# mLSTM state update, token scores and memory attention of a hybrid decoder step: ScalarE decay, grouped column-tiled products, zero-padded 64-row operands

## The chip, the cores and the metric

The kernel runs on one core of one Trainium2 chip. The metric is the time of one execution on the device, in microseconds (us); the median of three runs stands for a kernel. One profiled execution, with a record of every instruction, gives the views that are quoted below.

## The reference

One layer of a decoder serves 512 prompt rows and 8 decoding sequences of 4 new tokens each (32 sample rows) with the same weights; d_model is 1024 and everything is fp32. Cut to what matters here:

```python
# 1. hybrid mixer: mLSTM heads (4 x 128) beside differential attention (4 heads; q, k = 2 x 64, v = 128)
z = rms_norm(x) @ w_in
C_new = decay * C + (w * k)^T v          # mLSTM state, per sequence and head, 128 x 128
num   = w_inter * (q @ C) + s @ v        # the cached state is read before it is replaced
s     = einsum('bqhcd,bkhcd->bhcqk', q, k) * 64 ** -0.5      # c = 0, 1: two components of 64
p     = softmax(where(causal, s, -inf)); a = p[c=0] - lam * p[c=1]; o = a @ v
#    prompt: 512 keys; each sequence: 256 paged keys (2 pages) + its 4 new ones
x = x + rms_norm(concat(h_ml, h_da) @ w_out)
# 2. cross-attention, 4 heads x 256, into 256 memory tokens
#    prompt: k, v = mem_prompt @ w_mk, w_mv; each sequence: its own cached k, v (1 MB each)
x = x + rms_norm(softmax(q @ k^T / 16) @ v @ w_mo)
# 3. ConvFFN, d_ff = 2752 = 21.5 x 128
x = x + rms_norm((silu(g) * a) @ w_down)     # a, g: causal width-3 convolutions of x @ w_up
```

It returns the layer's output and the new caches and states.

## The kernel before, in words

**Units and queues.** TensorE (PE) does products and transposes, VectorE (DVE), ScalarE (ACT) and GpSimd (POOL) the rest; nearly all loads and stores are issued on one queue, SP's. The program is written in a tile framework: tiles come from pools with a fixed number of buffers, a new tile waits until its buffer's last user is done, and a planner orders each engine's instructions ahead of time from the program's order and its own estimate of when each becomes ready. `tc.issue_after(x)` holds the instructions in its block behind instruction x.

**Pools that the change touches.** S has 11 large tiles (transposed queries and keys, probabilities, padded operands). W has 4 slots of 128x2x1024; a slot holds one split weight tile, or one sequence's transposed keys (kT), or its values (vt). Stage (wst) has 6 buffers of 128x1024 for what is loaded. PSUM is shared by a pool of five banks (names mm, sda, ssc, tpa, oda, sca) and one of three (tpk, mlus, mlsi, cpt, spa and other short-lived results). T2, Z and N hold temporaries.

**Weights.** Each product with weights is done as three passes with operands split into a high and a low part: ACT casts the staged tile to the high part, DVE subtracts it for the low one (`split`, lines 142 and 143). `W.add` notes weight tiles in program order, `W.pump` loads and splits as many as there are slots (`W.nslots`), `W.get` and `W.free` pass them on. `slotA` makes a tile of 256 rows x 512 columns; the last 192 rows of w_down come as 128 and 64 rows, each split by itself.

**mLSTM states of the sequences (L948 to L964).** Step i of 8 is group g = i // 4 of four sequences and head i % 4. At the first step of a group, 16 products (32 query columns each, in one of four column tiles of PE) read that group's states into `pi` (mlsi). Then one matmul gives the four sequences' updates (mlus, 128x512), four DVE instructions do state = state * decay + update, and the state tile is stored. The state tiles sit in buffers that later stages load into.

**Token attention (L1139 to L1189 and the loop behind it).** For each sequence b, `dk_load` gathers two pages of keys, `dk_turn` transposes them (two tpk banks, one copied by ACT and one by DVE), `dk_scores` does four passes, one for each head, in column tiles of 32, and then the row maximum (DVE) and exp (ACT). Queries of both components lie side by side, zero-padded, in `qz`. A pipeline runs the three with one step of prompt attention between each two.

**Prompt attention.** `da_soft(i)` is block b = i // 4 of 128 queries and head i % 4. Component c lies in partitions 64c to 64c + 63 of `dqT` and `dkT`; its scores are one fp32 product over these 64 rows (two passes) and a bf16 matmul that adds the causal mask:

```python
rr = slice(64 * c, 64 * c + 64)
mm(sv[c], lhsT=dqT[rr, h, c0:c0 + P], rhs=dkT[rr, h, 0:nk], start=True, stop=False)
mm(sv[c][:, c0:nk], lhsT=identb, rhs=cmaskb, start=False, stop=True)
```

Maximum (DVE), exp (ACT) and the combination of both components (DVE) follow; `da_turn` transposes, `da_av` multiplies with the values. Fillers (`F`) with other work run between the steps.

**Memory attention (L1373 to L1450).** A half load i is 128 of a sequence's 256 keys, all heads. `mk_load` stages it, `mk_turn` transposes eight 128x128 blocks, `mk_scores` does a sequence's eight passes in column tiles of 32; `mv_load` loads a sequence's values into a slot of W, `mv_out` adds eight passes to `pso`. Generator `prompt` yields the prompt's own memory attention step by step: cpt and sca scores, and cpo outputs at line 1366. The order around it is written out:

```python
for b in range(NB):                  # NB = 8
    mk_scores(2 * b + 1)
    if b < 4:
        for j in (2 * b + 8, 2 * b + 9):
            mk_turn(j)
            if j + 6 < 2 * NB: mk_load(j + 6)
    else:
        mv_load(b - 4)
    if b % 2 == 1: next(prompt, None)
```

After the softmax the weight tiles of w_mo (`slotsA`, staged by line 227) are noted, sequences 4 to 7 get their `mv_load`, and `mv_out` runs from 0 to 7 with prompt steps between.

**ConvFFN.** Tiles of 128 of the 2752 features go through up projection, convolution and `gate`, then through w_down in groups; feature tile j = 21 has only 64 rows, so its products use 64 rows (`one`, L1645 to L1647, for prompt blocks; `sample_mm`, line 366, in column tiles of 32, for the sample rows).

## Time and profile before

| | |
|---|---|
| median of three runs (lowest, highest) | 990.26 us (988.76, 992.15) |
| the profiled execution, and its span | 989.55 us, 987.8 us |
| busy share of the span: PE, DVE, ACT, POOL | 97%, 61%, 39%, 20% |
| mean granted clock of TensorE | 0.993 of full speed |
| moved by DMA | 130.26 MB, 132 GB/s in the mean |

A profile line of the timeline has start and duration in us, engine, program line, operation, tile written <- tiles read, rows*columns of PE in use, shape, type, and xN where N like instructions in a row are put together; square brackets give the idle time before it and what ended that. A line of groups has busy time and mean ns of one behind the first bar, idle time before the group and its main releaser behind the second. A line by stretch has the stretch's length, then each engine's busy time and number of instructions, TensorE's granted clock, the busy share of the DMA engines and GB/s. PEld is TensorE's loading of the stationary operand, which can run beside products.

### The profile page before, as it was taken

To read this page: it belongs to the slowest core of one execution; us is meant where nothing else is said; L and a number is where in the kernel's file an instruction comes from. 1 tells how busy PE (TensorE), PEld (TensorE's weight loads), DVE (VectorE), ACT (ScalarE), POOL (GpSimd) and SP (SyncE) were. 2 spreads that over 40 slices of the span, in tenths; PEclk is the share of its full clock that TensorE was granted. 3 is DMA by queue.
4 is the path that set the end of the run, shared out by engine and by line. 5 is a ranking of instruction groups with operands and counts; after the bars stand their busy time and mean duration, and the time that the engine had idled before them with its cause. 6 is when DMAs were issued, how large, how long until landed. Compare 5 with 4: busy or idle time off the path is not lost.

```text
span 987.8 us, 17060 instructions
## 1 busy us (share of the span) xinstructions
PE 962.1 (97%) x6615; PEld 811.1 (82%) x6615; DVE 603.4 (61%) x1129; ACT 389.1 (39%) x746; POOL 195.5 (20%) x389
## 2 busy tenths in 40 slices
PE   8999999999999999999999999999999999999994
PEld 5899777789655878898767889989987997997983
DVE  6835325645786257633653569827757675685677
ACT  5754313334576357633543433342312222222232
POOL 6610000115231214400000354201100010110114
PEclk9999999999899999999999999999999999999998
DMA  8950222260835068765841764063053214304113
GB/s 283 301 161 1 86 75 91 63 206 12 255 109 177 21 219 266 261 219 168 304 171 49 233 197 127 6 171 86 4 139 103 74 42 117 118 26 141 31 47 112
DMA packets 120401, 130.26 MB, mean 132 GB/s; under 512 B 8423, under 2 KB 85832, under 8 KB 120320
## 3 DMA queue, kind: packets, MB, share of 16 engines
q1 hardware_dynamic: 114136, 125.69, 41.1%
q10 hardware_dynamic: 6184, 3.48, 1.2%
q8 instruction: 52, 0.85, 0.3%
q14 instruction: 29, 0.24, 0.1%
HBM read 112.22 MB, written 16.93 MB: 131 GB/s over the span
## 4 chain that ended last, share of the span: by engine, by line
PE 83%; DMA 6%; DVE 5%; issue 2%; ACT 2%; POOL 1%; SPq 1%; DVEq 0%; POOLq 0%; ACTq 0%
PE mm L455 30%; PE mm L386 5%; PE mm L387 5%; PE mm L388 5%; PE mm L443 5%; PE mm L1645 4%; PE mm L1647 4%; PE mm L1646 4%; PE mm L366 3%; PE sda L1180 2%; DMA xb<-x_d 2%; PE tpk L1385 2%; DMA xb<-in_x_prompt_dram 1%; DMA wst<-in_w_mk_dram 1%; PE cpo L1366 1%
## 5 line engine op out<-in xcount | busy, mean ns | idle before, releaser
L142 ACT CAST wslot<-wst 128x1024 fp32r<-128x1024 f32 (+1 forms) x127 | 131.0, 1036 | 273.3 <-issue 73.8
L455 PE MATMUL mm<-fT,wslot 128*128 128x256 f32 (+1 forms) x1872 | 235.7, 288 | 0.0
L455 PEld LDWEIGHTS mm<-fT,wslot 128*128 128x128 f32 x1872 | 234.7, 188 | 0.7 <-issue 0.4
L143 DVE TENSOR_TENSOR wslot<-wst,wslot 128x1024 fp32r<-128x1024 f32 (+1 forms) x127 | 154.9, 1222 | 91.8 <-ACT wslot L142 91.2
L1645 PE MATMUL mm<-wslot,act 128*128 128x512 f32 (+1 forms) x176 | 71.0, 405 | 0.0
L1646 PE MATMUL mm<-wslot,act 128*128 128x512 f32 (+1 forms) x176 | 69.5, 395 | 0.0
L1647 PE MATMUL mm<-wslot,act 128*128 128x512 f32 (+1 forms) x176 | 69.1, 397 | 0.0
L1546 POOL COPY cvo<-u 128x2 f32<-128x2 f32 x43 | 16.2, 377 | 221.3 <-DVE u L1544 221.3
L386 PE MATMUL mm<-wslot,hT 128*128 128x512 f32 x128 | 51.8, 407 | 0.0
L387 PE MATMUL mm<-wslot,hT 128*128 128x512 f32 x128 | 50.8, 397 | 0.0
L455 PE MATMUL mm<-hT,wslot 128*128 128x256 f32 (+1 forms) x384 | 50.7, 289 | 0.0
L388 PE MATMUL mm<-wslot,hT 128*128 128x512 f32 x128 | 50.6, 398 | 0.0
L455 PEld LDWEIGHTS mm<-hT,wslot 128*128 128x128 f32 x384 | 48.9, 188 | 0.5 <-issue 0.2
L1645 PEld LDWEIGHTS mm<-wslot,act 128*128 128x128 f32 (+1 forms) x176 | 33.4, 190 | 15.8 <-issue 7.8
L1541 DVE TENSOR_TENSOR u<-mm,rsb 128x256 f32<-128x256 f32 x43 | 18.1, 423 | 43.8 <-PE mm L455 43.8
L1647 PEld LDWEIGHTS mm<-wslot,act 128*128 128x128 f32 (+1 forms) x176 | 33.0, 188 | 7.7 <-issue 0.4
L1646 PEld LDWEIGHTS mm<-wslot,act 128*128 128x128 f32 (+1 forms) x176 | 33.1, 188 | 6.4
L1558 ACT ACTIVATE c<-c 128x560 f32<-128x560 f32 x21 | 14.1, 672 | 60.4 <-DVE c L1552 60.4
L1658 DVE TENSOR_TENSOR yp<-mm,yp 128x512 f32<-128x512 f32 x40 | 27.3, 688 | 13.7 <-PE mm L1647 13.6
L1552 DVE SCALAR_TENSOR_TENSOR c<-u,cvT,c 128x560 f32<-128x560 f32 x43 | 34.3, 797 | 0.8
L1551 DVE SCALAR_TENSOR_TENSOR c<-u,cvT,c 128x560 f32<-128x560 f32 x43 | 34.0, 792 | 0.1
L386 PEld LDWEIGHTS mm<-wslot,hT 128*128 128x128 f32 x128 | 24.1, 188 | 6.6 <-issue 2.1
(458 smaller groups left out, 1876.4 us busy)
## 6 DMA issues: line engine op xcount, KB each, us to landing
wst<-in_w_up_dram SPq DMA_DIRECT2D x42, 512.0 KB
wst<-in_w_in_dram SPq DMA_DIRECT2D x28, 512.0 KB
wst<-in_w_down_dram SPq DMA_DIRECT2D x20, 512.0 KB
wst<-in_cache_mem_k_dram SPq DMA_DIRECT2D x16, 512.0 KB
vt<-in_cache_mem_v_dram SPq DMA_DIRECT2D x8, 1024.0 KB
wst<-in_w_mk_dram SPq DMA_DIRECT2D x8, 512.0 KB
xb<-in_x_prompt_dram SPq DMA_DIRECT2D x8, 512.0 KB
wst<-in_cache_dk_dram SPq DMA_DIRECT2D x16, 256.0 KB
```

What stands on the lines that cost most here:

```text
L142: nc.scalar.copy(out=hi, in_=src)
L143: (eng or nc.vector).tensor_tensor(out=lo, in0=src, in1=f32(hi), op=SUB)
L386: mm(ps[b], lhsT=xt.hi(k, c0, c0 + n), rhs=s[:, 0, kk, :], start=(k == 0), stop=False)
L387: mm(ps[b], lhsT=xt.hi(k, c0, c0 + n), rhs=s[:, 1, kk, :], start=False, stop=False)
L388: mm(ps[b], lhsT=xt.lo(k, c0, c0 + n), rhs=s[:, 0, kk, :], start=False, stop=(k == nk - 1))
L443: mm(ps, lhsT=s[:, l, k, :], rhs=x(k, c0, c1), start=(k == 0 and j == 0), stop=(k == 7 and j == 2))
L455: mm(ps[i], lhsT=s[:, l, k, :], rhs=x(k, c0, c1), start=(k == 0 and j == 0), stop=(k == 7 and j == 2))
L1551: STT(out=c, in0=u[:, 1:EXT - 1], scalar=w[1], in1=c, op0=MUL, op1=ADD)
L1552: STT(out=c, in0=u[:, 0:EXT - 2], scalar=w[0], in1=c, op0=MUL, op1=ADD)
L1645: mm(ps, lhsT=t[:, 0, c0:c0 + P], rhs=s[:n, 0, i % 2, :], start=st, stop=False)
L1646: mm(ps, lhsT=t[:, 0, c0:c0 + P], rhs=s[:n, 1, i % 2, :], start=False, stop=False)
L1647: mm(ps, lhsT=t[:, 1, c0:c0 + P], rhs=s[:n, 0, i % 2, :], start=False, stop=en)
```

## The change

The state update reads all eight sequences' states ahead of the first update, lets ACT multiply by the decay and DVE add the whole bank. Prompt score products use all 128 rows: `dqz` is a copy of the queries with component 0's rows zero, and component 1's rows of `dqT` are cleared. Token scores are done for two sequences together, behind the second one's transposes. In the memory stage, scores of four sequences stand together twice, transposes 8 to 15 are held behind the first four, scores 4 to 7 behind the last transpose; values are loaded by halves, those of sequences 0, 1, 2 and 7 into staging buffers; outputs stand together as 0 to 3 and 4 to 7, with prompt steps between. Feature tile 21 and the last half tile of w_down are padded with zero rows to 128.

```diff
@@ -227,9 +227,10 @@
                 dma(out=st, in_=w[r0:r0 + 256, n0:n0 + 512].rearrange("(k p) n -> p k n", p=P))
                 split_w(sv, st, share)
             else:
+                nc.gpsimd.memset(st[nrow - P:, 1, :], 0.0)
                 for k, n in ((0, P), (1, nrow - P)):
                     dma(out=st[:n, k, :], in_=w[r0 + k * P:r0 + k * P + n, n0:n0 + 512])
-                    split(sv[:n, 0, k, :], sv[:n, 1, k, :], st[:n, k, :])
+                split(sv[:, 0], sv[:, 1], st)
             return sv, st
         W.add(emit)
 
@@ -948,16 +949,16 @@
     def mls_update(i):
         g, h = i // H, i % H
         cs_t = csts[g, h]
-        if h == 0:
-            for b in range(4):
+        if i == 0:
+            for b in range(NB):
                 for k in range(H):
-                    mm(pi[NS * k:NS * k + NS, 0:P], lhsT=qzm[:, 256 * k + (4 * g + b) * NS:256 * k + (4 * g + b + 1) * NS],
-                       rhs=csts[g, k][:, b, :], start=(g + b == 0), stop=(g == 1 and b == 3))
+                    mm(pi[NS * k:NS * k + NS, 0:P], lhsT=qzm[:, 256 * k + b * NS:256 * k + (b + 1) * NS],
+                       rhs=csts[b // 4, k][:, b % 4, :], start=(b == 0), stop=(b == NB - 1))
         pu = at("mlus")
         mm(pu, lhsT=kS[:, h, :], rhs=vzs[i], start=True, stop=True)
         for b in range(4):
-            STT(out=cs_t[:, b, :], in0=cs_t[:, b, :], scalar=dec[:, h, 4 + 4 * g + b:5 + 4 * g + b], in1=pu[:, b * P:(b + 1) * P],
-                op0=MUL, op1=ADD)
+            nc.scalar.mul(out=cs_t[:, b, :], in_=cs_t[:, b, :], mul=dec[:, h, 4 + 4 * g + b:5 + 4 * g + b])
+        VTT(out=cs_t, in0=cs_t, in1=v2(pu, P), op=ADD)
         dma(out=O["s_ml_C"][0, 4 * g:4 * g + 4, h].rearrange("b d e -> d b e"), in_=cs_t)
         F.run(2.5)
 
@@ -1142,6 +1143,14 @@
         rr = slice(64 * c, 64 * c + 64)
         nc.gpsimd.tensor_copy(out=qz[rr, :, :, c, :], in_=dqT[rr, :, SEQ:].rearrange("p h (g r) -> p h g r", g=2))
 
+    dqz = S([P, H, SEQ], F32, "dqz")
+    nc.gpsimd.memset(dqz[0:64], 0.0)
+    for b in range(4):
+        c = slice(b * P, b * P + P)
+        nc.scalar.copy(out=dqz[64:128, :, c], in_=dqT[64:128, :, c])
+        nc.gpsimd.memset(dqT[64:128, :, c], 0.0)
     kst, kts, pts, aTs, outs, rcs = {}, {}, {}, {}, {}, {}
 
     def dk_load(b):
@@ -1149,6 +1158,8 @@
         kst[b] = [st[:, 0:512], st[:, 512:1024]]
         for g in range(2):
             gather("cache_dk", b, g, kst[b][g])
+    turned = {}
 
     def dk_turn(b):
         kt = kts[b] = wp.tile([P, H, 260], F32, name="kT", tag="W")
@@ -1156,16 +1167,22 @@
         for g in range(2):
             ps = at("tpk")
             for h in range(H):
-                tr(ps[:, h * P:(h + 1) * P], kst[b][g][:, h * P:(h + 1) * P], ident)
+                turned[b] = tr(ps[:, h * P:(h + 1) * P], kst[b][g][:, h * P:(h + 1) * P], ident).ins
             (VCP if g else nc.scalar.copy)(out=kt[:, :, g * P:(g + 1) * P], in_=v2(ps, P))
 
     def dk_scores(b):
-        ps = mmp("ssc")[:, :260]
-        for h in range(H):
-            mm(ps[NS * h:NS * h + NS], lhsT=qz[:, h, b // 4].rearrange("p c r -> p (c r)"), rhs=kts[b][:, h, :],
-               start=True, stop=True)
-        VTT(out=ps[:, 256:260], in0=ps[:, 256:260], in1=con("cm4"), op=ADD)
-        sample_exp(sall, b, ps, nm, su)
+        if b % 2 == 0:
+            return
+        ps = {c: mmp("ssc")[:, :260] for c in (b - 1, b)}
+        with tc.issue_after(turned[b]):
+            for c in (b - 1, b):
+                for h in range(H):
+                    mm(ps[c][NS * h:NS * h + NS], lhsT=qz[:, h, b // 4].rearrange("p c r -> p (c r)"), rhs=kts[c][:, h, :],
+                       start=True, stop=True)
+        for c in (b - 1, b):
+            VTT(out=ps[c][:, 256:260], in0=ps[c][:, 256:260], in1=con("cm4"), op=ADD)
+            sample_exp(sall, c, ps[c], nm, su)
 
     def da_soft(i):
         b, h = i // H, i % H
@@ -1176,8 +1193,7 @@
         su = small(2, "su")
         sv = [mmp("sda")[:, :nk] for _ in range(2)]
         for c in range(2):
-            rr = slice(64 * c, 64 * c + 64)
-            mm(sv[c], lhsT=dqT[rr, h, c0:c0 + P], rhs=dkT[rr, h, 0:nk], start=True, stop=False)
+            mm(sv[c], lhsT=(dqz if c else dqT)[:, h, c0:c0 + P], rhs=dkT[:, h, 0:nk], start=True, stop=False)
             mm(sv[c][:, c0:nk], lhsT=identb, rhs=cmaskb, start=False, stop=True)
         for c in range(2):
             VRED(out=nm[:, c:c + 1], in_=sv[c], axis=AX.X, op=MAX, negate=True)
@@ -1382,28 +1398,34 @@
         for q in range(2):
             ps = at("tpk")
             for j in range(4):
-                tr(ps[:, j * P:(j + 1) * P], kst[i][:, (4 * q + j) * P:(4 * q + j + 1) * P], ident)
+                t = tr(ps[:, j * P:(j + 1) * P], kst[i][:, (4 * q + j) * P:(4 * q + j + 1) * P], ident)
             (VCP if q else nc.scalar.copy)(out=kts[b][:, 4 * q:4 * q + 4, c * P:(c + 1) * P], in_=v2(ps, P))
-    def mk_scores(i):
-        b, c = i // 2, i % 2
-        if c == 0:
-            return
+        return t.ins
+    def mk_scores(b):
         ps = mmp("ssc")[:, :256]
         for c in range(2):
             for h in range(H):
-                mm(ps[NS * h:NS * h + NS], lhsT=qs[:, 2 * h + c], rhs=kts[b][:, 2 * h + c, :], start=(c == 0), stop=(c == 1))
+                t = mm(ps[NS * h:NS * h + NS], lhsT=qs[:, 2 * h + c], rhs=kts[b][:, 2 * h + c, :], start=(c == 0), stop=(c == 1))
         sample_exp(sall, b, ps, nm, su)
+        return t.ins
 
     def mv_load(b):
-        vts[b] = wp.tile([P, 2, DM], F32, name="vt", tag="W")
-        dma(out=vts[b], in_=I["cache_mem_v"][0, b].rearrange("(c p) h d -> p c (h d)", p=P))
+        if 2 < b < 7:
+            t = wp.tile([P, 2, DM], F32, name="vt", tag="W")
+            vts[b] = [t[:, 0], t[:, 1]]
+        else:
+            vts[b] = [stage(), stage()]
+        for c in range(2):
+            dma(out=vts[b][c], in_=I["cache_mem_v"][0, b, c * P:(c + 1) * P].rearrange("t h d -> t (h d)"))
 
     def mv_out(b):
         for c in range(2):
             for h in range(H):
-                mm(pso[NS * h:NS * h + NS], lhsT=az[c][:, h, b * NS:(b + 1) * NS], rhs=vts[b][:, c, 256 * h:256 * h + 256],
-                   start=(b == 0 and c == 0), stop=(b == NB - 1 and c == 1))
+                t = mm(pso[NS * h:NS * h + NS], lhsT=az[c][:, h, b * NS:(b + 1) * NS], rhs=vts[b][c][:, 256 * h:256 * h + 256],
+                       start=(b == 0 and c == 0), stop=(b == NB - 1 and c == 1))
+        return t.ins
 
     sall = S([P, NB, 256], F32, "cas")
     nm, su = small(NB, "snm"), small(NB, "ssu")
@@ -1416,17 +1438,26 @@
             for j in (i // 2 - 1, i // 2):
                 mk_turn(j)
                 mk_load(j + 6)
-    for b in range(NB):
-        mk_scores(2 * b + 1)
-        if b < 4:
-            for j in (2 * b + 8, 2 * b + 9):
-                mk_turn(j)
-                if j + 6 < 2 * NB:
-                    mk_load(j + 6)
-        else:
-            mv_load(b - 4)
-        if b % 2 == 1:
-            next(prompt, None)
+    next(prompt)
+    for b in range(4):
+        t = mk_scores(b)
+    with tc.issue_after(t):
+        for j in range(8, 16):
+            t = mk_turn(j)
+            if j + 6 < 2 * NB:
+                mk_load(j + 6)
+            if j == 11:
+                next(prompt)
+    for b in range(3):
+        mv_load(b)
+    next(prompt)
+    with tc.issue_after(t):
+        for b in range(4, NB):
+            t = mk_scores(b)
+    for b in range(3, 7):
+        mv_load(b)
+    next(prompt)
     _, az = sample_softmax(sall, su, None, con("selX"), "ca")
     for _ in range(NMID):
         next(prompt, None)
@@ -1434,14 +1465,15 @@
     for n0 in (0, 512):
         slotsA(w_mo, n0)
     W.nslots = NSLOT
-    for b in range(NB):
-        if b >= 4:
-            mv_load(b)
+    for b in range(4):
+        mv_out(b)
+        if b == 0:
+            mv_load(7)
     W.pump()
-    for b in range(NB):
+    next(prompt, None)
+    next(prompt, None)
+    for b in range(4, NB):
         mv_out(b)
-        if b in VSTEPS:
-            next(prompt, None)
     run(prompt)
     oS = Z("oS")[:, :256]
     nc.scalar.copy(out=oS, in_=pso)
@@ -1560,16 +1592,18 @@
             cg = T2([64, EXT - 2], "cg")
             ACT(out=cg, in_=ua.c[64:128], func=AF.Silu)
         ca = ua.c
-        a = T2([P, ROWS], "a")[:n]
-        VTT(out=a[:, :SEQ], in0=ca[:n, :SEQ], in1=cg[:n, :SEQ], op=MUL)
+        a = T2([P, ROWS], "a")
+        if n < P:
+            nc.gpsimd.memset(a[n:], 0.0)
+        VTT(out=a[:n, :SEQ], in0=ca[:n, :SEQ], in1=cg[:n, :SEQ], op=MUL)
 
         def sv(c):
             return c[:n, SEQ:].rearrange("p (b j) -> p b j", j=6)[:, :, 2:6]
-        VTT(out=v2(a[:, SEQ:], TS), in0=sv(ca), in1=sv(cg), op=MUL)
-        split(act[i // 2][:n, i % 2, 0, :], act[i // 2][:n, i % 2, 1, :], a)
+        VTT(out=v2(a[:n, SEQ:], TS), in0=sv(ca), in1=sv(cg), op=MUL)
+        split(act[i // 2][:, i % 2, 0, :], act[i // 2][:, i % 2, 1, :], a)
         t = sm.tile([P, NS], F32, name="acs", tag="acs", bufs=5)
-        nc.gpsimd.tensor_copy(out=t[:n], in_=a[:, SEQ:])
-        return t[:n]
+        nc.gpsimd.tensor_copy(out=t, in_=a[:, SEQ:])
+        return t
 
     gf = gbc("g_ffn_post")
     acts, acss = {}, {}
@@ -1629,8 +1663,7 @@
         behind = []
 
         def one(b, ps, i, s):
-            n = P if js[i] < 21 else 64
-            t = act[i // 2][:n, i % 2]
+            t = act[i // 2][:, i % 2]
             st, en = i == 0, i == nk - 1
             if b == 4:
 
@@ -1642,9 +1675,9 @@
                 return
             s = s[0]
             c0 = b * P
-            mm(ps, lhsT=t[:, 0, c0:c0 + P], rhs=s[:n, 0, i % 2, :], start=st, stop=False)
-            mm(ps, lhsT=t[:, 0, c0:c0 + P], rhs=s[:n, 1, i % 2, :], start=False, stop=False)
-            mm(ps, lhsT=t[:, 1, c0:c0 + P], rhs=s[:n, 0, i % 2, :], start=False, stop=en)
+            mm(ps, lhsT=t[:, 0, c0:c0 + P], rhs=s[:, 0, i % 2, :], start=st, stop=False)
+            mm(ps, lhsT=t[:, 0, c0:c0 + P], rhs=s[:, 1, i % 2, :], start=False, stop=False)
+            mm(ps, lhsT=t[:, 1, c0:c0 + P], rhs=s[:, 0, i % 2, :], start=False, stop=en)
 
         def add_y(b, ps, n0):
             c = slice(n0, n0 + 512)
```

## The prediction

> **What bounds the kernel now.** I read the page's busy table first, then the chain that ended last, then busy time by stretch for the stages the diff touches, then TensorE's timeline there.
>
> ```profile
> PE 962.1 (97%) x6615; PEld 811.1 (82%) x6615; DVE 603.4 (61%) x1129; ACT 389.1 (39%) x746; POOL 195.5 (20%) x389
> ...
> PE 83%; DMA 6%; DVE 5%; issue 2%; ACT 2%; POOL 1%; SPq 1%; DVEq 0%; POOLq 0%; ACTq 0%
> ```
>
> TensorE (PE) is busy 97% of the span and carries 83% of the chain. So a microsecond of PE work removed is a microsecond of time, unless another engine or a load is close behind in that stage.
>
> ```profile
> core 0: us, PE busy (x) PEld busy (x) DVE busy (x) ACT busy (x) POOL busy (x), PEclk, DMA share, GB/s
> 240.00:250.00 10.00, 10.00 (x105) 9.41 (x106) 7.21 (x22) 1.33 (x3) 7.07 (x9) 1.00 0.18 55
> 250.00:257.00 7.00, 5.37 (x56) 3.39 (x58) 5.69 (x24) 4.23 (x12) 0.92 (x2) 0.96 0.67 192
> 257.00:262.00 5.00, 4.57 (x31) 3.53 (x29) 3.27 (x13) 1.74 (x5) 0.75 (x2) 0.50 1.01 290
> 262.00:275.00 13.00, 12.33 (x99) 7.96 (x91) 10.83 (x30) 9.30 (x31) 6.08 (x8) 0.95 0.80 263
> 275.00:295.00 20.00, 20.00 (x129) 11.77 (x127) 15.54 (x46) 14.86 (x49) 5.46 (x6) 1.00 0.35 112
> 300.00:321.00 21.00, 21.00 (x209) 11.90 (x209) 14.85 (x26) 14.38 (x33) 2.02 (x3) 1.00 0.62 208
> 470.00:485.00 15.00, 15.00 (x135) 10.15 (x134) 9.97 (x24) 8.44 (x29) 0.00 (x0) 1.00 0.89 297
> 485.00:513.00 28.00, 28.00 (x242) 19.01 (x241) 16.98 (x41) 14.31 (x47) 0.00 (x0) 1.00 0.71 260
> ```
>
> The stages are: cached states (240 to 258), prompt and token attention (251 to 322), memory attention (457 to 518). Read here how much room VectorE (DVE) and ScalarE (ACT) leave: much in the memory stage, little in 262 to 295, where DVE is busy 26.4 of 33.
>
> **Prompt score queries over 128 rows.** A component's score is two passes of 64 rows, then a mask matmul of 128 rows.
>
> ```profile
> 280.03 0.70 PE L1180 MATMUL sda<-dkT,dqT 64*128 64x256 f32 x2
> 280.66 0.23 PE L1181 MATMUL sda<-cb 128*128 128x128 bf16 x1
> 280.82 0.70 PE L1180 MATMUL sda<-dkT,dqT 64*128 64x256 f32 x2
> ...
> 270.95 0.23 PE L1181 MATMUL sda<-cb 128*128 128x128 bf16 x1
> 271.01 1.04 PE L1159 MATMUL tpk<-cpk,wst 128*128 128x128 f32 x8
> ...
> 432.48 1.47 PE L1385 MATMUL tpk<-cpk,wst 128*128 128x128 f32 x12
> 433.70 2.50 PE L455 MATMUL mm<-hqT,wslot 128*128 128x256 f32 x18
> ```
>
> Start to start, one component of 256 keys takes 0.63 + 0.16 = 0.79 us. Passes of 128 columns that stay at 128 rows start every 0.10 (12 in 1.22), and a mask followed by a 128-row instruction lasts 0.06. Padded, the same component should take 4 x 0.10 + 0.06 = 0.46 to 0.49, so 0.30 less; the part lost is the two changes of row mode and a weight load that isn't hidden, and doesn't grow with the keys. With 16 head blocks of two components: 32 x 0.30 = 9.5 us of PE.
>
> The Trainium skill speaks against this edit: "TensorEngine Tiling (Array Packing)", section Performance Considerations, recommends row tiling for a contraction of 64 or less, up to twice as fast, since tiles work in parallel. If the two components ran so side by side now, padding would cost instead of gain; the starts above (0.79 apart, the mask between) show them one after the other, so by the rule the sum would lose this term, by the trace it keeps it.
>
> Preparing the padded copy:
>
> ```profile
> 289.80 1.81 POOL L1027 MEMSET daz<- 128x2048 f32 x1
> ...
> L1208 ACT ACTIVATE dao<-oda,rc 128x128 f32<-128x128 f32 x16 | 5.5, 368 | 1.3 <-PE oda L1206 1.0
> L959 DVE SCALAR_TENSOR_TENSOR wst<-wst,dec,mlus 128x128 f32<-128x128 f32 x32 | 8.9, 341 | 3.0 <-PE mlus L957 2.9
> L1386 DVE COPY kT<-tpk 128x512 f32<-128x512 f32 x16 | 11.0, 689 | 12.8 <-PE tpk L1385 12.8
> ```
>
> POOL clears 2048 columns (1.81) and four quarters of that again (1.8); ACT copies four times 512 columns, some 0.7 each by DVE's 0.69 for such a tile. POOL is free 9.0 of the 17 us from 240 to 257, ACT 11.4. The queries are finished before that stage, and the new tile takes a buffer that the prompt recurrence has left, so I cost it at nothing; uncovered, the first score would wait for one clear, one copy and a quarter's clear, 1.8 + 0.7 + 0.5 = 3 us. It is the eleventh live tile of eleven buffers, so a later one could wait; none is due before the prompt blocks end.
>
> **Cached states.** 32 DVE operations of 0.34 (10.9) become 8 of 0.69 (5.5); ACT gets 32 products of at most 0.37 (11.8). ACT has 11.4 us free from 240 to 257, but may start only after all 64 state reads, about 243, and its queue also holds the gate's sigmoids and the first exps, and the state tiles must be stored before token keys can be gathered into their buffers. So DVE's wait gives way to ACT's: between 1.6 gained (the idle PE of 250 to 257) and 3.4 lost (11.8 less the 8.4 that ACT has free from 243 to 257). I take 0.5 lost: nearer the middle than either end, since DVE, on which PE waits there now, is relieved of 5.4 in the same place. If ACT is late, what waits next is the store of the state tiles, and behind it the gathers on SP's queue and the transposes of the token keys. The state reads in one group instead of two save one trip into column mode, 0.3 (below).
>
> **Trips into column mode.** Token scores, memory scores and memory outputs use four 32-column tiles at once.
>
> ```profile
> 480.32 0.62 PE L1395 MATMUL ssc<-kT,qs 128*32 128x256 f32 x4
> 480.88 0.66 PE L1354 MATMUL cpt<-cpk,cp 128*128 128x128 f32 x4
> ...
> 508.42 1.93 PE L1405 MATMUL pso<-vt,caz 128*32 128x256 f32 x32
> 510.28 1.67 PE L1366 MATMUL cpo<-pT,mvN 128*128 128x512 f32 x6
> ...
> L1395 PE MATMUL ssc<-kT,qs 128*32 128x256 f32 x128 | 11.9, 386 | 0.0
> L1405 PE MATMUL pso<-vt,caz 128*32 128x256 f32 x128 | 9.6, 385 | 0.0
> ```
>
> Four passes take 0.56 until the next instruction, 32 take 1.86: a round of up to eight costs 0.43, a trip 0.13 more, and about 0.2 for the change in and out (the price that the rows of the feature tiles below show). Token scores in pairs: four trips fewer, 1.3. Memory scores: 128 passes, now scattered among transposes, busy 11.9; as two groups of 64, each 1.93 + 4 x 0.43 = 3.65, busy 7.3: 4.6 saved. Outputs likewise 9.6 to 7.3: 2.3. The changes of mode around the groups that vanish add some 1.8. Memory stage together: 8.7.
>
> **What moves in the memory stage.** Transposes 8 to 15 are held behind the scores of sequences 0 to 3, scores 4 to 7 behind the last transposes. Each of the eight blocks (8 x 0.10 of PE) needs one DVE copy (0.69) and one on ACT before its buffer is free. The row maxima of four sequences and a prompt block's softmax come on top, so DVE has about as much to do there as PE, and nothing else of PE's may pass: I put 1 us of waiting on it (an estimate from these two rates, 0.8 against 0.7 a block), none if the maxima wait, 3 if each block waits for its copy (8 x 0.4). SP issues sixteen half loads of values instead of eight, three sequences into staging buffers as the keys leave them, four into weight slots, the last after the first output.
>
> ```profile
> 469.00 1.25 SPq L227 DMA_DIRECT2D wst<-in_w_mo_dram  x2
> ...
> 509.56 1.05 ACT L142 CAST wslot<-wst 128x1024 fp32r<-128x1024 f32 x1 [0.38 <-PE pso L1405]
> ...
> 483.88 3.09 PE L1366 MATMUL cpo<-pT,mvN 128*128 128x512 f32 x12
> ```
>
> What this delays: w_mo's tiles, now staged from 469 and waiting 40 us for a slot, can be staged only when outputs 1 and 2 free staging buffers. Behind the last value load (1 MB) the first 0.5 MB lands some 6 us after output 0 at the stage's 260 GB/s, then come the cast (1.05) and the subtraction: 8 to 9. PE then still has outputs 1 to 3 (2.7), two prompt outputs (3.1 each by the row) and outputs 4 to 7 (3.65) to do, 12.5 with nothing for scores and transposes: covered, by some 4 us. Without that cover it costs up to 9. Values of sequences 3 to 6 need slots that the scores of 4 to 7 free; 4 MB at 260 GB/s are 16 us, about what the softmax and the prompt blocks between take in the trace. I take 7.0 of the 8.7: 1 for the block of transposes, 0.7 for such loads.
>
> **Padded feature tiles (j = 21).**
>
> ```profile
> 751.13 1.18 PE L366 MATMUL mm<-wst,acs 128*32 128x256 f32 x8
> 752.24 0.50 PE L1645 MATMUL mm<-wslot,act 128*128 128x512 f32 x1
> ...
> 753.27 0.39 PE L1646 MATMUL mm<-wslot,act 128*128 128x512 f32 x1
> 753.50 0.40 PE L1647 MATMUL mm<-wslot,act 128*128 128x512 f32 x1
> 753.83 0.49 PE L1645 MATMUL mm<-wslot,act 64*128 64x512 f32 x1
> 754.16 0.39 PE L1646 MATMUL mm<-wslot,act 64*128 64x512 f32 x1
> ...
> 766.37 0.50 PE L1645 MATMUL mm<-wslot,act 64*128 64x512 f32 x1
> ```
>
> Steps of 0.23 become 0.33 twice at each change between 128 and 64 rows: 0.2 a change. From 753.83 to 766.37 the timeline has twelve; all vanish: 2.4. Eight sample passes with a 64-row half take 1.11; in one mode they are a round of 0.56: 0.55 in each of two halves, 1.1. Two casts and two subtractions fall away, two POOL clears come. PE alone works there: 3.4 saved, hardly in doubt.
>
> **The sum.** PE work removed: 9.5 + 1.3 + 0.3 in attention, 8.7, 3.4, together 23.2. Attention won't keep it all. Of the 32 components (counted in the timeline) 17 lie in 262 to 295: they and the pairs would shorten 33 us to 26.6, where DVE alone needs 26.4, in a chain of maximum, exp, product and transpose; I take 3.3. Nine lie in 300 to 321, with DVE at 14.85: 2.0 of 2.7. The rest lie where PE already idles: 0.7. So 6.0 + 7.0 + 3.4 - 0.5 = 15.9. The profiled execution took 989.55 (span 987.8, the rest around it), 0.7 under the median 990.26: 974.
>
> **Rivals.**
> - All is realised (13%): 23.2, and the half-clock stretch goes too.
>
> ```profile
> 255.83 0.47 PE L957 MATMUL mlus<-vz,kS 128*128 128x512 f32 x1 [1.07 <-DVE wst L959]
> 257.94 3.67 PE L1159 MATMUL tpk<-cpk,wst 128*128 128x128 f32 x16 [0.43 <-ACT numS L969]
> ```
>
> There 16 transposes take 3.67 where 0.10 to 0.12 each (1.75) is usual, the granted clock being 0.50: 2 to 2.5 us. Against: DVE's 26.4. Time 990 - 25.5, 964.5.
> - Engines behind PE become the bound (20%): attention gives 2, the memory stage 3 because forced order makes PE wait for copies and loads, features 3.4: 982. For it: DVE and ACT in 262 to 295; against: DVE is busy 10 of 15 at most in the memory stage.
> - The change hardly does what it says (8%): the groups are split again by the order that the planner finds, and the padded scores wait for DVE anyway; the features alone remain, 987 (or nothing, 990). For it: outputs 4 to 7 and 0 to 3 are grouped in the program's order only; against: the scores are held together by an explicit order.
> - Slower (7%): the clock. It fell after PE had been busy 5.37 of 7 us, and each fall costs about 2.5 us per 6.8. With less PE work and the same DVE chain, attention may sit below the point where the clock is held. Eight falls, some 54 of the 71 us of attention, decide: 974 + 20 = 994; the whole stretch, ten, gives 999. Against: 275 to 295 has the full clock with many short waits. The Trainium skill ("TensorE: Matmul & The Clock Gate", HAM oscillation) ties the fall to idle gaps above some 3.4 us; here it came after gaps of at most 1.07, so the measurement decides, and by the page's rule this rival would be out, its 7% with the main case.
>
> **Numbers.** The main case has 52%, 969 to 979. With the two beside it, 965 to 984, 85%. About 0.3% (3 us) is what a measurement of this kernel tells from no change: faster 0.86 (the three, and one in eight of the case that does little), same 0.07, slower 0.07.
>
> **What would show it.** A component of 256 keys start to start at 0.49, and no 64-row score in the trace. Memory scores in two groups, busy near 7.3; outputs in two. ACT products between the state reads and 256. Features stretch without 0.33 steps. Wrong if PE idles more than 5 us in attention or in the memory stage, if ACT ends what the states wait for, or if w_mo's first cast ends later than the last prompt output.

## The result, and the profile after

The changed kernel takes 976.86 us (median of 4, 975.66 to 979.82) against 990.82 for the kernel before (4 runs): ratio 0.9865 [0.9836, 0.9894]. Timed once more later it gave 0.9862 [0.9841, 0.9882]. The forecast was 974 (965 to 984). The square brackets hold the 95% interval of a ratio; the kernel before was timed beside each group of runs, and since its median went from 990.6 to 992.1 between them, it is the ratios that are compared below. Its profiled execution took 975.66 with a span of 973.9, 13.9 under that of before, where the sum had said 15.9.

From the page of the changed kernel, the busy table and the chain by engine:

```profile
PE 947.7 (97%) x6615; PEld 815.0 (84%) x6615; DVE 595.8 (61%) x1103; ACT 401.0 (41%) x782; POOL 199.8 (21%) x397
...
PE 82%; DMA 5%; DVE 5%; ACT 4%; issue 2%; POOL 1%; SPq 0%; ACTq 0%; DVEq 0%; POOLq 0%
```

PE stays the bound and has as many instructions as before, with 14.4 us less busy time. ACT's share of the chain doubled, from 2% to 4%. To see where the time came from I took the start of the same PE instruction in both timelines:

| PE instruction | before | after | difference | gained in the stretch |
|---|---|---|---|---|
| first product with w_out | 320.94 | 314.45 | -6.49 | 6.5: states and attention |
| last product of the memory queries | 455.61 | 447.87 | -7.74 | 1.3: a wait ahead of it |
| last product with w_mo | 567.97 | 556.24 | -11.73 | 4.0: memory stage |
| first transpose of convolution rows (cvo) | 624.40 | 614.06 | -10.34 | -1.4: clock |
| last product with w_down | 974.57 | 960.59 | -13.98 | 3.6: features |

The 1.3 us are one wait of PE for a normalisation on ACT, 1.5 in this record of before and 0.2 in this one of after; in the twelve other records, of all variants, it lies between under 0.3 and 1.8, so it isn't the change's. A record is the profiled execution of a run.

**Attention.** The timeline of PE, first two single token scores with transposes between them, then the score components of a head block of 256 keys and a pair of token scores:

```profile
262.99 0.65 PE L1181 MATMUL ssc<-kT,qz 128*32 128x260 f32 x8
263.56 1.09 PE L1170 MATMUL tpk<-cpk,wst 128*128 128x128 f32 x8
264.59 0.65 PE L1181 MATMUL ssc<-kT,qz 128*32 128x260 f32 x8
...
276.52 0.60 PE L1196 MATMUL sda<-dkT,dqT 128*128 128x256 f32 x2
276.95 0.22 PE L1197 MATMUL sda<-cb 128*128 128x128 bf16 x1
277.01 0.65 PE L1196 MATMUL sda<-dkT,dqz 128*128 128x256 f32 x2
...
277.65 1.08 PE L1181 MATMUL ssc<-kT,qz 128*32 128x260 f32 x16
```

A component takes 0.43 + 0.06 = 0.49 from start to start, as forecast (0.46 to 0.49), where it took 0.79; over the four sizes of 128 to 512 keys the saving is 0.24 to 0.30. Two sequences' scores stand in one trip of 16 passes, but in two of the four pairs only: the other two pairs are split by transposes of a later sequence, as above. So there are six trips, not the four of the forecast. A whole pair takes 1.01 us from start to the next instruction, two single scores 1.16 at full clock. The stretch from 240 to 321 us, before and after, and the falls of the clock in the record of after:

```profile
240.00:321.00 81.00, 77.67 (x645) 50.25 (x645) 60.90 (x167) 49.12 (x146) 24.86 (x33) 0.96 0.52 165
```

```profile
240.00:321.00 81.00, 74.61 (x675) 54.56 (x675) 59.57 (x149) 63.43 (x188) 29.72 (x38) 0.96 0.52 165
...
255.68:262.51 6.83, 4.26 (x20) 3.75 (x21) 2.72 (x11) 5.29 (x12) 1.47 (x3) 0.51 0.98 309
559.47:566.29 6.82, 6.66 (x30) 6.37 (x31) 6.48 (x11) 2.27 (x6) 4.62 (x8) 0.51 0.97 274
```

In the same 81 us PE is idle 6.4 instead of 3.3. The second line of after is the clock's fall that was there before; the third, at the start of the up projection, is not in the record of before, and is the 1.4 us lost in the table. Twelve of the fourteen records have such a fall there, for 3.41 or 6.83 us, those of single parts too; only the kernel before and E3 below do not. So it isn't shown to be the change's. The two longest waits of attention are these, 3.4 us where the kernel before waits three times for 2.1:

```profile
255.92 1.11 PE L1170 MATMUL tpk<-cpk,wst 128*128 128x128 f32 x4 [1.11 <-DVE wst L961]
259.36 1.97 PE L1170 MATMUL tpk<-cpk,wst 128*128 128x128 f32 x8 [2.32 <-ACT numS L970]
```

and ACT's groups from 240 to 262 tell why:

```profile
L960 ACT ACTIVATE wst<-wst,dec 128x128 f32<-128x128 f32 x32 | 9.5, 387 | 0.0
L989 ACT ACT_TABLE_LOAD x2 | 2.6, 1283 | 0.0
L1200 ACT ACT_TABLE_LOAD x2 | 2.6, 1283 | 0.0
```

The 32 products take 9.5 us in one piece, and the sigmoids of the gate (L989) and the exps (L1200), now squeezed in behind them, alternate, so that ACT loads its function table four times in this stretch. The kernel before has one load here and one, at 234.56, ahead of it; over the whole kernel it is ten loads instead of eight, so the alternation costs two more, 2.6 us of ACT. The copy of numS, for which the second group of transposes waits, stands behind all that. (The Trainium skill, "ScalarE: Activation LUTs", What ACT_TABLE_LOAD costs, gives 1283 ns for such a load; the trace agrees. The drain of some 1380 ns that the section adds is not in this trace: the next row begins 0.01 us behind the load's end.)

**Memory stage.** PE's rows of scores (L1409), of outputs (L1426), and the transposition behind them:

```profile
450.82 1.05 PE L1409 MATMUL ssc<-kT,qs 128*32 128x256 f32 x10
452.39 3.22 PE L1409 MATMUL ssc<-kT,qs 128*32 128x256 f32 x54
466.44 3.66 PE L1409 MATMUL ssc<-kT,qs 128*32 128x256 f32 x64
484.29 0.62 PE L1426 MATMUL pso<-wst,caz 128*32 128x256 f32 x2
485.31 2.58 PE L1426 MATMUL pso<-wst,caz 128*32 128x256 f32 x43
490.92 1.48 PE L1426 MATMUL pso<-vt,caz 128*32 128x256 f32 x18
493.00 0.63 PE L1426 MATMUL pso<-vt,caz 128*32 128x256 f32 x4
495.15 1.06 PE L1426 MATMUL pso<-vt,caz 128*32 128x256 f32 x12
497.69 0.85 PE L1426 MATMUL pso<-vt,caz 128*32 128x256 f32 x11
...
500.88 0.44 PE L1482 MATMUL ost<-cpk,oS 128*128 128x128 f32 x2 [0.67 <-ACT oS L1479]
```

The scores are three groups instead of twelve: from each group's start to the next instruction 0.99 + 3.15 + 3.59 = 7.7 against 11.0 before, 3.3 gained. The outputs are still six groups (rows with vt and wst that follow each other are one): 0.55 + 3.59 + 1.41 + 0.55 + 0.98 + 1.86 = 8.94 against 8.94 in nine groups before, nothing gained. A wait of 0.67 for ACT's copy of the outputs is new.

**Features.** The rows that were 64 high are 128 high and follow each other in 0.23; the eight sample passes take 0.57:

```profile
747.12 0.64 PE L367 MATMUL mm<-wst,acs 128*32 128x256 f32 x8
747.69 0.51 PE L1678 MATMUL mm<-wslot,act 128*128 128x512 f32 x1
748.04 0.40 PE L1679 MATMUL mm<-wslot,act 128*128 128x512 f32 x1
748.27 0.40 PE L1680 MATMUL mm<-wslot,act 128*128 128x512 f32 x1
```

### The profile page after: what moved, and what is told of

It reads as the page before. It is cut to its first block, busy times and chain, and to the rows that moved or that the text cites. A ratio compares the mean times of both kernels' runs of the same rounds, so it can differ in the third digit from the quotient of the medians.

```text
span 973.9 us, 17096 instructions
## 1 busy us (share of the span) xinstructions
PE 947.7 (97%) x6615; PEld 815.0 (84%) x6615; DVE 595.8 (61%) x1103; ACT 401.0 (41%) x782; POOL 199.8 (21%) x397
## 4 chain that ended last, share of the span: by engine, by line
PE 82%; DMA 5%; DVE 5%; ACT 4%; issue 2%; POOL 1%; SPq 0%; ACTq 0%; DVEq 0%; POOLq 0%
PE mm L456 31%; PE mm L444 8%; PE mm L387 5%; PE mm L389 5%; PE mm L388 5%; PE mm L1678 4%; PE mm L1680 4%; PE mm L1679 4%; PE mm L367 3%; DMA wst<-in_w_mo_dram 1%; PE sda L1196 1%; DVE xb L1111 1%; PE tpk L1401 1%; DMA xb<-in_x_prompt_dram 1%; DMA xb<-x_d 1%
## 5 line engine op out<-in xcount | busy, mean ns | idle before, releaser
L142 ACT CAST wslot<-wst 128x1024 fp32r<-128x1024 f32 x125 | 130.8, 1050 | 270.3 <-issue 80.2
L143 DVE TENSOR_TENSOR wslot<-wst,wslot 128x1024 fp32r<-128x1024 f32 x125 | 153.5, 1231 | 93.3 <-ACT wslot L142 92.8
L1678 PE MATMUL mm<-wslot,act 128*128 128x512 f32 x176 | 69.8, 398 | 0.0
L1679 PE MATMUL mm<-wslot,act 128*128 128x512 f32 x176 | 69.6, 395 | 0.0
L1680 PE MATMUL mm<-wslot,act 128*128 128x512 f32 x176 | 69.1, 397 | 0.0
L1678 PEld LDWEIGHTS mm<-wslot,act 128*128 128x128 f32 x176 | 33.5, 190 | 11.9 <-issue 4.5
L1680 PEld LDWEIGHTS mm<-wslot,act 128*128 128x128 f32 x176 | 33.1, 188 | 7.7 <-issue 0.4
L1679 PEld LDWEIGHTS mm<-wslot,act 128*128 128x128 f32 x176 | 33.1, 188 | 6.9
```

Of the source, the lines that this page charges most:

```text
L142: nc.scalar.copy(out=hi, in_=src)
L143: (eng or nc.vector).tensor_tensor(out=lo, in0=src, in1=f32(hi), op=SUB)
L1678: mm(ps, lhsT=t[:, 0, c0:c0 + P], rhs=s[:, 0, i % 2, :], start=st, stop=False)
L1679: mm(ps, lhsT=t[:, 0, c0:c0 + P], rhs=s[:, 1, i % 2, :], start=False, stop=False)
L1680: mm(ps, lhsT=t[:, 1, c0:c0 + P], rhs=s[:, 0, i % 2, :], start=False, stop=en)
```

## The experiments

**One part alone, on the kernel before.** E1 has the padding of the prompt scores:

```diff
+    dqz = S([P, H, SEQ], F32, "dqz")   # and its clears and copies
-            mm(sv[c], lhsT=dqT[rr, h, c0:c0 + P], rhs=dkT[rr, h, 0:nk], start=True, stop=False)
+            mm(sv[c], lhsT=(dqz if c else dqT)[:, h, c0:c0 + P], rhs=dkT[:, h, 0:nk], start=True, stop=False)
```

> The kernel before with the padded prompt scores alone (128 rows instead of 64; the states, the token scores, the memory stage and the features as before). Theory, PE bounds the attention stage: 32 components lose 0.30 each, 9.5 us of PE work; DVE and ACT hold some back, so 5 to 7 us of time, near 984. Rival, DVE and ACT are the bound there: 2 us or less, 988 or more. Rival by the rule of row tiling (64-row passes of both components run side by side): slower than before. Start to start of a component of 256 keys: 0.49 in either of the first two.

Measured: 983.95 (6 runs) against 990.68, ratio 0.9930 [0.9908, 0.9952]. The first product with w_out starts at 313.53, 7.4 earlier than before. PE has as little idle time in 240 to 321 as before, 3.6 us:

```profile
240.00:321.00 81.00, 77.41 (x682) 55.70 (x681) 61.55 (x173) 52.06 (x155) 29.92 (x38) 0.96 0.52 165
```

From 220 us, where both records stand level within 0.1 us, to that product, PE is busy 89.9 of 93.5 us against 97.3 of 100.9 before, with the same 807 products: 7.4 us of work less and no more idle time. So the work that padding removes is nearer 7.4 than 9.5, and in this record DVE and ACT hold back none of it. The rival of little effect falls, and so does that of row tiling.

E2 has the memory stage alone:

```diff
+    for b in range(4):
+        t = mk_scores(b)
+    with tc.issue_after(t):
+        for j in range(8, 16):
...                                    # all of the change from mk_turn to run(prompt)
```

> The kernel before with the new memory stage alone. Theory, from the two traces: the scores' groups save 3.3 us of PE (11.1 to 7.7) and about 1.5 in changes of mode, the outputs save nothing because the planner splits them into six groups, 0.7 is lost to a wait for the copy of pso: 4 us, near 986. Rival, the forced order or the loads cost more and the 4 us come from attention's shift: under 2 us. Rival of the prediction: 7 us, 983.

Measured: 987.57 (12 runs), ratio 0.9966 [0.9953, 0.9980], 3.4 us. In its trace the last w_mo product gains 3.3 us on the last memory query. The score and output groups are those of the changed kernel (10, 54 and 64 scores), the wait for the copy of the outputs is 1.36. The prediction's 7 falls outside the interval (2.0 to 4.7 us).

E3 has the padded feature tile alone:

```diff
-                    split(sv[:n, 0, k, :], sv[:n, 1, k, :], st[:n, k, :])
+                split(sv[:, 0], sv[:, 1], st)
...
-            mm(ps, lhsT=t[:, 0, c0:c0 + P], rhs=s[:n, 0, i % 2, :], start=st, stop=False)
+            mm(ps, lhsT=t[:, 0, c0:c0 + P], rhs=s[:, 0, i % 2, :], start=st, stop=False)
```

> The kernel before with padded feature tile 21 alone. Theory: 12 changes of row mode at 0.2 and two groups of sample passes at 0.55, so 3.4 to 3.6 us less, near 987, and nothing else moves. Rival, part of the 3.6 us seen in that stretch comes from elsewhere (the place of the clock's fall): under 2.5 us.

Measured: 987.89 (12 runs), ratio 0.9975 [0.9959, 0.9991], 2.5 us with 3.4 inside the interval; in its trace the features stretch, from the first cvo to the last w_down product, is 3.65 shorter, as in the changed kernel (3.64).

E4 has the state update alone:

```diff
+            nc.scalar.mul(out=cs_t[:, b, :], in_=cs_t[:, b, :], mul=dec[:, h, 4 + 4 * g + b:5 + 4 * g + b])
+        VTT(out=cs_t, in0=cs_t, in1=v2(pu, P), op=ADD)
```

> The kernel before with the new state update alone (products on ACT, one bank addition on DVE, one group of state reads). Theory, ACT's start behind all reads takes the place of DVE's wait: 0 to 2 us slower, 990 to 992, with waits of PE before the token keys' transposes of 2 to 3.5 us (3.4 in the changed kernel). Rival, DVE's relief counts: 1 to 2 us faster.

Measured: 992.81 (12 runs), ratio 1.0028 [1.0012, 1.0045]: slower by 2.8. PE waits once, for a state tile. PE, then DVE:

```profile
259.38 2.90 PE L1159 MATMUL tpk<-cpk,wst 128*128 128x128 f32 x13 [3.12 <-DVE wst L960]
```

```profile
258.55 0.17 DVE L1186 RECIPROCAL rc<-su 128x2 f32<-128x2 f32 x1 [2.77 <-ACT pda L1184]
258.63 0.69 DVE L960 TENSOR_TENSOR wst<-wst,mlus 128x512 f32<-128x512 f32 x1
```

ACT's 32 products had ended at 251.9. What was late were the exps of the first head blocks, because sigmoids and exps alternate here too (ten table loads); the last bank addition stands behind a reciprocal that waits for them in DVE's queue. E10 below has the same update, with other score products and without the alternation (eight loads), and there the three waits before these transposes are 0.33, 0.43 and 0.80.

Yet from the first state read to the first w_out product its trace is only 0.3 longer than before, with a shorter stretch of half clock (3.41 us instead of 6.83). The rival, 1 to 2 us faster, falls. Another 1.0 of its record's 1.5 lies ahead of the up projection, in a wait of which E5 tells more. Whether that belongs to this edit is open.

**Parts taken out of the changed kernel.** E5 is the changed kernel again, E6 has the old state update in it, E12 the token scores of one sequence at a time.

> The changed kernel itself, timed on the same chip as the next three so that they can be compared with it. Theory, its time follows the stages of the trace: 976 to 978. In its own record I expect again a wait of 3 to 3.5 us in all before the token keys' first transposes, and the up projection to begin 2.4 or 3.6 us after the last w_mo product (2.4 in three of the records so far, 3.5 to 3.7 in three), which would show that this second wait is not the change's.

Measured: 976.88 (5 runs). In its record the two waits before the token keys' transposes are 1.11 and 2.68, 3.8 in all, a little over what I expected, and the up projection begins 2.5 after the last w_mo product. That second distance comes in two sizes, 1.6 to 2.5 in seven of the fourteen records and 3.1 to 3.7 in seven, and no single edit divides the one from the other.

```diff
-            nc.scalar.mul(out=cs_t[:, b, :], in_=cs_t[:, b, :], mul=dec[:, h, 4 + 4 * g + b:5 + 4 * g + b])
-        VTT(out=cs_t, in0=cs_t, in1=v2(pu, P), op=ADD)
+            STT(out=cs_t[:, b, :], in0=cs_t[:, b, :], scalar=dec[...], in1=pu[:, b * P:(b + 1) * P], op0=MUL, op1=ADD)
...                                    # and the state reads in two groups
```

> The changed kernel with the state update of before (four DVE instructions a step, two groups of state reads). Theory, the update on ACT starts behind all state reads and is what the token keys wait for: 1 to 2.5 us faster than the changed kernel, 974.5 to 976, and the wait of 2.3 us before the first transposes of token keys gone or under 1. Rival, DVE's relief pays for it: same or slower than the changed kernel.

Measured: 976.40 (5 runs), ratio to before 0.9860 [0.9841, 0.9878], against 0.9862 for E5: the same, as the rival had it. The 2.3 us wait is gone, but shorter ones like those of before are back (1.08, 0.57, 0.69, 0.42 here), and one of 0.81 at a later head block. Its record has no fall of the clock in attention, where E5's has one of 6.83 us, so the records can't say what the old update itself is worth there.

```diff
-        if b % 2 == 0:
-            return
-        ps = {c: mmp("ssc")[:, :260] for c in (b - 1, b)}   # and so on: dk_scores as before
```

> The changed kernel with the token scores one sequence at a time, as before. Theory: four trips into column mode come back, 1.3 us of PE work, of which up to 1.3 is time: 977 to 978.5. Rival, holding the scores of two sequences behind the second's transposes costs as much in waits (0.4 us before the scores at 272): no change, or slightly faster without it.

Measured: 978.98 (6 runs), ratio 0.9876 [0.9851, 0.9900]. Against 0.9862 that is 1.4 us slower; the first w_out product comes 2.3 later than in the changed kernel's first record, 0.3 of which was there at 220 us. But only two trips come back (eight instead of six), 0.3 us of PE in themselves and some 0.7 with the changes of mode at the prediction's price, so more than half of this is something else: PE waits 7.1 us from 220 us to that product instead of 6.4. The intervals of the times overlap widely: a gain from the pairs is likely, not shown.

**The outputs held together.** E7 undoes the planner's split by an explicit order:

```diff
+    with tc.issue_after(last[0]):          # last[0]: the latest PE instruction of the prompt steps
+        for b in range(4):
+            t = mv_out(b)
...
+    with tc.issue_after(t):
+        next(prompt, None)
+        next(prompt, None)
...                                          # the same for outputs 4 to 7 and run(prompt)
```

> The changed kernel with its memory outputs held together: outputs 0 to 3 behind the last prompt instruction issued so far, the next prompt steps behind them, and so again for 4 to 7. Theory, the planner's split into six groups ate the 2.3 us forecast for the outputs: busy time of the output passes from about 9 to 7.5, and 2 to 3 us of time less than the changed kernel. Rival, the split is where PE would else wait for values and copies: PE's idle time in this stage grows by what the groups save, no gain or a loss.

Measured: 978.99 (6 runs), ratio 0.9888 [0.9867, 0.9910]: 2.6 us slower than E5 by the ratios, whose intervals overlap. The outputs are three groups and take 7.7 from start to next instead of 8.9, but what follows them waits. PE and then ACT:

```profile
500.38 1.05 PE L1427 MATMUL pso<-wst,caz 128*32 128x256 f32 x16
501.36 0.66 PE L1371 MATMUL cpt<-cpk,cp 128*128 128x128 f32 x4
505.33 0.44 PE L1487 MATMUL ost<-cpk,oS 128*128 128x128 f32 x2 [3.33 <-ACT oS L1484]
```

```profile
503.01 1.99 ACT L142 CAST wslot<-wst 128x1024 fp32r<-128x1024 f32 x2
504.91 0.37 ACT L1484 COPY oS<-pso 128x256 f32<-128x256 f32 x1
```

The copy of the outputs stands behind two casts of w_mo on ACT, and PE has nothing left but what waits for ACT. The planner's mixture had covered this: the rival is right. In the groups 1.2 is gained, and the wait for the copy is 3.33 instead of 0.67 (1.02 in E5); from the last memory query to the last w_mo product it takes 109.6 us instead of 108.4 (108.5).

**The two components side by side.** The rule of row tiling that spoke against padding was set aside in the prediction because the components ran one after the other with the mask between. E8 moves the mask, on the kernel before:

```diff
             mm(sv[c], lhsT=dqT[rr, h, c0:c0 + P], rhs=dkT[rr, h, 0:nk], start=True, stop=False)
+        for c in range(2):
             mm(sv[c][:, c0:nk], lhsT=identb, rhs=cmaskb, start=False, stop=True)
```

> The kernel before with one edit: a head block's two 64-row score products are issued one after the other, both masks behind them; the planner leaves them next to each other in 5 of 16 head blocks. By the rule of row tiling, products on different row halves run in parallel: the second component's first pass starts at once with the first's last (well under the 0.32 us that a pass of 256 columns takes at 64 rows). Theory of the prediction, they run one after the other: start to start 0.3 (256 columns), only one change of row mode per block is saved, 1 to 1.5 us at most over these blocks, total 989 to 991.

Measured: 988.02 (10 runs), ratio 0.9972 [0.9959, 0.9984]. PE's rows of two head blocks of 512 keys, the first with its components apart, the second with both together (x4):

```profile
300.79 1.12 PE L1180 MATMUL sda<-dkT,dqT 64*128 64x512 f32 x2
301.85 0.23 PE L1182 MATMUL sda<-cb 128*128 128x128 bf16 x1
302.00 1.12 PE L1180 MATMUL sda<-dkT,dqT 64*128 64x512 f32 x2
303.06 0.23 PE L1182 MATMUL sda<-cb 128*128 128x128 bf16 x1
...
305.42 1.13 PE L1180 MATMUL sda<-dkT,dqT 64*128 64x512 f32 x4
306.48 0.29 PE L1182 MATMUL sda<-cb 128*128 128x128 bf16 x2
```

Four passes take the 1.06 us of two; the second component's first pass starts 7 ns behind the first's. So the rule of the Trainium skill ("TensorEngine Tiling (Array Packing)", Performance Considerations) holds here, up to the factor of two, once the products stand next to each other. My expectation that they would run in turn was wrong. E9 puts all 16 blocks so, E10 does it in the changed kernel instead of padding, E11 with the old states as well:

```diff
+        t = mm(sv[1][:, 0:1], lhsT=identb[64:128, :], rhs=cmaskb[64:128, 0:1], start=True, stop=True).ins
+        with tc.issue_after(t):
+            t = mm(sv[0], lhsT=dqT[0:64, h, c0:c0 + P], rhs=dkT[0:64, h, 0:nk], start=True, stop=False).ins
+        with tc.issue_after(t):
+            t = mm(sv[1], lhsT=dqT[64:128, h, c0:c0 + P], rhs=dkT[64:128, h, 0:nk], start=True, stop=False).ins
+        with tc.issue_after(t):        # both masks
```

> The kernel before with both components' 64-row products next to each other in all 16 head blocks: a one-column product on the upper row half takes the second bank first, the first component is issued behind it, the second behind the first, both masks behind that. Theory, after the runs in parallel seen where 5 blocks had it (starts 7 ns apart): a pair of 256 keys takes 0.32 + 0.31 + 0.13 = 0.77 instead of 1.58, over all blocks some 11 to 12 us of PE work less, against 9.5 by padding; so at least as fast as padding alone (983.95 on the other chip time), 981 to 984. Rival, DVE and ACT bound what attention can give: no better than padding. Rival, the forced order makes PE wait for two free banks at once: slower than padding by over 2 us.

> The changed kernel with the padding of the prompt scores taken out (no padded copy of the queries, no clearing) and the adjacent 64-row pairs of the run above in its place. Theory: PE work 2 to 4 us less than with padding, ACT's four copies and POOL's clears gone: 1 to 3 us faster than the changed kernel, 974 to 976. Rival, the attention stage is at the limit of DVE and ACT (idle PE in it is 6 us already): same as the changed kernel, PE's idle time there grows by what is saved.

> As the run above, with the state update of before as well. Theory: the states are worth nothing either way in company (the changed kernel with the old update took 976.4 against 976.9), so the same as the run above within 1 us. Rival, with ACT's products gone the adjacent pairs find ACT free earlier: 1 to 2 us faster.

Measured, with 992.11 for the kernel before on that chip: E9 990.32 (12 runs), ratio 0.9976 [0.9955, 0.9997]; E10 979.83 (6 runs), 0.9882 [0.9857, 0.9908]; E11 981.69 (6 runs), 0.9903 [0.9874, 0.9932]. E9 is slower than padding alone (0.9930, E1) by more than 2 us, as its last rival had it, and E10 is not faster than the changed kernel: both theories failed. E11, expected within 1 us of E10, is 2.1 slower by the ratios, whose intervals overlap. E9 has PE's work of the pairs about halved and gains a third of what padding gains. Its stretches, and PE's longest waits in them:

```profile
292.85:296.26 3.41, 3.06 (x13) 2.49 (x15) 1.45 (x5) 1.13 (x9) 0.25 (x1) 0.51 0.00 0
316.74:320.16 3.42, 3.42 (x10) 1.66 (x9) 2.24 (x4) 1.27 (x4) 2.81 (x4) 0.51 0.00 0
240.00:321.00 81.00, 72.76 (x670) 49.17 (x670) 62.28 (x173) 49.08 (x151) 28.09 (x37) 0.92 0.52 165
```

```profile
291.92 0.44 PE L1037 MATMUL spt<-cpk,spc 128*128 128x128 f32 x2 [1.22 <-ACT spc L1034]
293.20 0.40 PE L1237 MATMUL npn<-cpk,pz 128*32 128x128 f32 x1 [0.84 <-DVE pz L1234]
...
315.19 0.33 PE L1268 MATMUL dat<-cpk,dasq 128*128 128x128 f32 x1 [1.84 <-DVE dasq L1266]
```

PE is idle 8.2 of the 81 us, 4.6 more than with padding, waiting for DVE and ACT, and the clock fell twice more, for 3.41 us each, right behind such waits: its first w_out product comes at 318.44, 4.9 later than in E1. So the further PE work that is saved here turned into waits for DVE and ACT, and the clock took its share. Whether the forced order or the adjacency itself makes the waits was not separated. E8, with five blocks adjacent and nothing forced, gained 5.6 from the first state read to w_out, but with the full clock all through: the kernel before has 6.83 us of half clock there, with PE busy for 6.0 of it, so up to 3.0 of the 5.6 may be the clock's. E10 reaches that product at 318.34, 3.9 later than the changed kernel, of which 1.1 was there at 220 us, behind a fall of the clock at 97 us, ahead of all that differs. None of the variants beats the changed kernel by its interval.

## Why the prediction was right, and which terms were off

- **Padded scores** (9.5 of PE, of which attention keeps part): the component's 0.49 is as forecast. Alone the part is worth 6.9 to 7.4 (E1), and there nothing is held back: the 9.5 was too large, and so was what DVE and ACT were to keep of it. With the token pairs and the states the forecast was 6.0 - 0.5 = 5.5; the stage gained 6.5 in the first record and 5.4 in the second (E5), which was 1.2 behind at 220 us, with the fall at 97 us ahead of it. The 6.5 are 1.0 less than padding alone gains in E1's record: from 220 us to the first w_out product PE is busy 88.1 of 94.5 us, so against E1 the pairs and the states took 1.8 off PE's busy time and added 2.8 of idle time. That 5.5 and 6.5 lie close is in part luck: the work removed by padding and the part of it held back were both put too high, and the one made up for the other. PE idles 6.4 us in attention, over the 5 that I had named as a sign of being wrong; the sign was right that engines behind PE held it up, and set too low, since the work removed was larger than the idle time added.
- **Token pairs** (1.3): six trips instead of four, so about half of it. That a transpose could go between the two scores of a pair was not in the working: the order given holds the start of a pair, and nothing keeps other work out of it.
- **States** (0.5 lost, between 1.6 gained and 3.4 lost): ACT does end what the states wait for, another of my signs of being wrong, but not by the products: 32 took 9.5 us and were done by 252.4. The exps behind them were late, by two more table loads, 2.6 us of ACT, that were not in the working (E4). Alone the part loses 2.8; in company it is worth nothing either way within the intervals (E6).
- **Memory stage** (8.7 of PE, 7.0 realised): it gave 4.0, and this is the term that was most mis-sized. The step that failed is "outputs likewise 9.6 to 7.3: 2.3" with its share of the mode changes: the outputs stayed in six groups and gained 0.0. That the planner may split the groups stood only in a rival, for all of the stage; the scores, which an explicit order holds, came as three groups and gave 3.3 of 4.6. Part of that gap is the measure: the 4.6 was taken from busy times, 11.9 to 7.3, and by starts they had been 11.0. The feared waits for the transposes' copies and for the loads didn't come; a wait of 0.67 for the copy of the outputs did. And in E7 forcing the groups, done in that one way, did not give the 2.3.
- **Features** (3.4): 3.6, the rows as forecast.
- **Clock**: the rival had it fall eight times in attention; in this record it fell once more behind the start-up, at the up projection, and cost 1.4. E9 and E10 show the rival's mechanism in attention, with two more falls and one more.
- **The sum**: 15.9 forecast against 13.9, from -3.0 (memory), +1.0 (attention and states), +0.2 (features), and -0.1 from what isn't shown to be the change's (1.3 gained by a shorter wait, 1.4 lost by the clock). So the main case and its bound, PE, were right, and the errors of the terms partly cancelled. The four parts alone (E1 to E4) add up to 10.0 by their ratios, where the whole gained 13.4; their intervals together are wide enough for that, and the token pairs were not run alone.

## What to carry to other kernels

Grouping products that need a mode of PE saves what the trips cost only where the group stays whole. The memory scores stayed nearly whole, where the order held them and also held back the transposes that would have gone between; the token pairs, of which only the start was held, were split in two of four, and the outputs, grouped in the program's order alone, into six. So look at the planner's order first, and ask what covers the wait behind the group. Where the engine behind the bound is busy three quarters of a stage and in one chain with it (DVE 62 of 81 us in E9), price each further saving on the bound by that engine: the adjacent pairs take PE less time than padding does and gained a third as much. Moving work to a second engine adds its position in that engine's queue, and there the function tables of ScalarE count as work where the new order makes functions alternate.

## What the runs showed of the hardware

- Two fp32 products on different row halves, next to each other in PE's queue, start 7 ns apart and run side by side; with one bf16 instruction of 128 rows between them they ran one after the other (1.21 us from start to start at 512 keys, 300.79 to 302.00 in E8). Padding to 128 rows is second best by PE work (0.98 for a pair of 256 keys by the rows of after, 0.76 side by side, from 269.96 to 270.72 in E9) but was the best in time here.
- The clock fell to half in multiples of 3.41 us, with the longest gap of PE ahead of it between none (at 97 us in five records, among small products, PE busy throughout) and 3.1 us; in the record of E6 stretches with waits of 1.08, 0.57 and 0.69 in attention passed with the full clock, and so did a wait of 3.33 us in E7. No single length of wait fits these; what decides stays open. That fall of 3.41 us cost 1.5: E3, 0.2 behind the kernel before at 66 us, is 1.65 behind at the first state read, with the same instructions between. At the up projection a fall of 3.41 us cost less: from the last w_mo product to the first cvo E5, with one, takes 56.6 us, and the kernel before, with none, 56.4.
